# Attention scores of two heads as 64-row tiles, in an encoder layer on one core of a Trainium2 chip

## The chip, the cores and the metric

The kernel runs on one core of one Trainium2 chip. The metric is the device time in microseconds of one execution of the whole program. Shorter is better. The times of several executions are compared by their median, and a profiled execution shows where the time goes.

A core has five engines, each with its own queue of instructions that it works off in order: PE (TensorE, matrix products and transposes), DVE (VectorE), ACT (ScalarE), POOL (GpSimd) and SP (SyncE, which here issues the DMAs). They wait for one another through semaphores. PE multiplies a stationary operand (the weights, loaded by an instruction of its own, shown as PEld) with a moving operand that streams past it, and writes to PSUM, which has eight banks.

## The reference

One layer of an encoder is computed for two groups of 1024 rows, x_prompt and x_sample, with shared weights; everything is in 32-bit floats. Per group:

```python
h = rms_norm(x, norm_g) * (1 + scale) + shift          # scale, shift, gate from silu(c) @ w_ada + b_ada
qa, ka, va, za, qb, kb, vb, zb, ga, gb = split(h @ w_in)
# A: 8 query heads, 2 key/value heads of 64; RMS norm of q and k per head, 2-D rotary positions
oa = softmax(qa @ ka.T / 8) @ va * silu(za)             # query head j uses key/value head j // 4
# B: 4 heads, two 64-wide softmax maps each, values of 128
ob = (softmax(q0 @ k0.T / 8) - lam * softmax(q1 @ k1.T / 8)) @ vb
ob = rms_norm(ob, subln_g) * (1 - lam_init) * silu(zb)
merged = sigmoid(ga) * (oa @ w_proj_a) + sigmoid(gb) * (ob @ w_proj_b)
y = x + gate * (merged @ w_out)
```

The score products contract over 64 numbers only, the width of a head.

## The kernel before

PE multiplies 32-bit numbers in a rounded format here (float32r in the code). To keep the accuracy, the kernel splits an operand into an exact high part and a low part, the rest: `x = hi + lo`. A product of two split operands is then hi·hi + hi·lo + lo·hi, three matmuls that add up in one PSUM bank. The projections (`proj_tt`, L432, and `z_gen`, L594) do this over eight chunks of 128 rows.

**Scores before.** A head is 64 wide, so its high and low parts together fill 128 partitions. `pairs_T` (L472) transposes a pair of heads (L479) and writes, for each head, one tile with the high part on one half of the partitions and the low part on the other: two ACT copies (L481) and two DVE subtractions (L482), each on 64 partitions. For the keys `swap_halves` (L496) makes a second copy in which the halves have changed places, with POOL (L501). `softmax_unit` (L607) then takes 128 queries of one head: for each half of the 1024 keys it multiplies the stacked query tile with the stacked keys (hi·hi + lo·lo, L617) and with the swapped ones (hi·lo + lo·hi, L618), both over all 128 rows of the array, into one bank of the pool `ps_s`, which has two buffers. DVE takes the row maximum from it (L619), ACT the exponential and its sum (L620). The two halves are brought together by small operations on DVE, ACT and POOL (L621 to L625).

**What follows the scores.** `a_scores` (L628) and `b_scores` (L641) scale the exponentials (L637, L653, L660) into tiles of the pool `ppool`, six buffers of 128 x 1024. `pT_pieces` (L665) transposes them on PE (L671), splits them (L674, L675), and the value products follow (L686 and L687 for branch A, L713 for B). `attention` (L739) computes the scores of a unit, then the values of the unit before. In branch A a unit is one head and 256 queries, in branch B one head (two maps) and 256 queries.

**The order of the work.** Generators yield after each step, and `weave` (L60) lays several of them beside each other at given shares: in six phases per group (two for branch A, four for B) the attention runs beside the projections that the next phase needs and beside pieces of the gate paths (`z_gen`), which keep PE supplied. A scheduler in the tile framework then takes the instructions, with their dependences, and fixes the final order of each engine's queue when the program is built. In group 0, phase 5, `gate_gen` (L375) adds small products with only two output rows (L383).

`load_w` (L154) brings 256 columns of a weight matrix with one DMA for each half (L162) where they are contiguous, and splits them on ACT and POOL. Two such weight tiles are held.

Of the kernel before, what the change touches and what calls it, by code (L numbers as in the profile page):

```python
# [78 lines left out]
def kernel(ctx: ExitStack, tc: tile.TileContext, t: dict):  # L79
# [74 lines left out]
    def load_w(pieces):  # L154
        """pieces(half) -> the columns of four contraction chunks, 256 in all"""
# [32 lines left out]
    def row_scale(xt):  # L188
        """1 / rms of the rows"""
# [117 lines left out]
    def mod_rows():  # L307
        """the second group's shift and scale, as rows in DRAM"""
# [14 lines left out]
    def ht0(ht):  # L323
        """the modulation of the first group's transposed rows, and their split"""
# [128 lines left out]
    def rope(x3, s3, cos, sin, half):  # L453
        """x3 = x3*cos + swap(x3)*sin; s3 is scratch"""
# [15 lines left out]
    LO, HI = slice(0, 64), slice(64, 128)  # L470

    def pairs_T(x3, even, odd):  # L472
        """Transpose pairs of heads; the exact parts of the first of each pair go to even (high
        part in the lower partitions), those of the second to odd (high part in the upper ones)."""
# [5 lines left out]
        for dst, hi, lo in ((even, LO, HI), (odd, HI, LO)):  # L480
            nc.scalar.activation(dst[hi], ps[hi], AF.Copy)  # L481
            nc.vector.tensor_tensor(out=dst[lo], in0=ps[hi], in1=dst[hi].bitcast(F32), op=ALU.subtract)  # L482
# [13 lines left out]
    def swap_halves(dst, srcs, tq):  # L496
        """dst = the sources with their partition halves swapped, over half of the positions"""
        sl = slice(tq * 512, (tq + 1) * 512)
        for i, src in enumerate(srcs):
            for a, b in ((LO, HI), (HI, LO)):  # L500
                nc.gpsimd.tensor_scalar(  # L501
                    out=dst[a, i, sl], in0=src[b, sl].bitcast(F32),
                    scalar1=1.0, scalar2=1.0, op0=ALU.mult, op1=ALU.mult,
                )

# [3 lines left out]
    def kva_gen(ht, out):  # L509
        w = kva_w.pop() if kva_w else load_w(w_cols(w_in, (C_KA, 256)))  # L510
        k1, k2 = v2(utile()), v2(utile())
        va = utile().rearrange("p (n k d) -> p n k d", n=NTT, k=2)
        out["k1"], out["k2"], out["va"] = k1, k2, va
# [11 lines left out]
        def back(tt, x3):  # L525
            sl = slice(tt * P, (tt + 1) * P)
            pairs_T(x3, k1[:, 0:1, sl], k1[:, 1:2, sl])
            if tt % 4 == 3:
                swap_halves(k2, (k1[:, 0], k1[:, 1]), tt // 4)
# [3 lines left out]
    def qa_gen(ht, out, half):  # L533
        w = load_w(w_cols(w_in, (C_QA + half * 256, 256)))
# [15 lines left out]
    def qkb_gen(ht, out, h):  # L550
        w = load_w(w_cols(w_in, (C_QB + h * P, P), (C_KB + h * P, P)))
        qk, k2 = (v2(utile()), v2(utile())), v2(utile())
        out[h] = (qk, k2)
# [8 lines left out]
        def back(tt, x3):  # L562
            sl = slice(tt * P, (tt + 1) * P)
            pairs_T(x3, qk[0][:, :, sl], qk[1][:, :, sl])
            if tt % 4 == 3:
                swap_halves(k2, (qk[0][:, 1], qk[1][:, 1]), tt // 4)
# [40 lines left out]
    def softmax_unit(q, k1, k2, qt, pt, f):  # L607
        """Scores of 128 queries: each half of the keys goes to pt as exp(scores - the half's maximum);
        f gets the factor of each half that makes the row's softmax of it"""
        qsl = q[:, qt * P : (qt + 1) * P]  # L610
        m = tiny.tile([P, 2], F32, tag="m", name=nm("m"))
        su = tiny.tile([P, 2], F32, tag="su", name=nm("su"))
        mm = tiny.tile([P, 1], F32, tag="mm", name=nm("mm"))
        for n in range(2):
            s = ps_s.tile([P, 512], F32, tag="s", name=nm("s"))
            sl = slice(n * 512, (n + 1) * 512)
            nc.tensor.matmul(s, qsl, k1[:, sl], start=True, stop=False)  # L617
            nc.tensor.matmul(s, qsl, k2[:, sl], start=False, stop=True)  # L618
            nc.vector.tensor_reduce(out=m[:, n : n + 1], in_=s, axis=AX.X, op=ALU.max, negate=True)  # L619
            nc.scalar.activation(pt[:, sl], s, AF.Exp, bias=m[:, n : n + 1], accum_out=su[:, n : n + 1])  # L620
        nc.vector.tensor_tensor(out=mm, in0=m[:, 0:1], in1=m[:, 1:2], op=ALU.min)  # L621
        nc.scalar.activation(f, m, AF.Exp, scale=-1.0, bias=mm)  # L622
        nc.gpsimd.tensor_tensor(out=su, in0=su, in1=f, op=ALU.mult)  # L623
        nc.gpsimd.tensor_tensor(out=mm, in0=su[:, 0:1], in1=su[:, 1:2], op=ALU.add)
        nc.gpsimd.tensor_tensor(out=mm, in0=mm, in1=mone, op=ALU.pow)  # L625
        return mm

    def a_scores(u):  # L628
        q, k1, k2, pr = u["q"], u["k1"], u["k2"], u["pr"]
        u["p"] = []  # L630
        for i in range(2):
            pt = ptile()
            f = tiny.tile([P, 2], F32, tag="r", name=nm("r"))
            r = softmax_unit(q, k1, k2, pr * 2 + i, pt, f)
            for n in range(2):
                half = pt[:, n * 512 : (n + 1) * 512]
                nc.gpsimd.tensor_scalar(out=half, in0=half, scalar1=f[:, n : n + 1], scalar2=r, op0=ALU.mult, op1=ALU.mult)  # L637
            u["p"].append(pt)
            yield 1

    def b_scores(u):  # L641
        u["p"] = []
        for i in range(2):
            qt = u["pr"] * 2 + i
            p0, p1 = ptile(), ptile()
            f0 = tiny.tile([P, 2], F32, tag="r", name=nm("r"))
            f1 = tiny.tile([P, 2], F32, tag="r", name=nm("r"))
            for m, (pt, f) in enumerate(((p0, f0), (p1, f1))):
                r = softmax_unit(u["qk"][m][:, 0], u["qk"][m][:, 1], u["k2"][:, m], qt, pt, f)
                if m == 0:  # L650
                    for n in range(2):
                        half = p0[:, n * 512 : (n + 1) * 512]
                        nc.gpsimd.tensor_scalar(  # L653
                            out=half, in0=half, scalar1=f0[:, n : n + 1], scalar2=r, op0=ALU.mult, op1=ALU.mult
                        )
                yield 1
            nc.gpsimd.tensor_scalar(out=f1, in0=f1, scalar1=r, scalar2=nlam, op0=ALU.mult, op1=ALU.mult)  # L657
# [5 lines left out]
            u["p"].append(p0)  # L663

    def pT_pieces(u):  # L665
        for cc in range(4):
            ps = tbank().rearrange("p (c n) -> p c n", c=2)
            for c in range(2):
                k = (cc * 2 + c) * P
                for i in range(2):  # L670
                    nc.tensor.transpose(ps[:, c, i * P : (i + 1) * P], u["p"][i][:, k : k + P], ident)  # L671
# [6 lines left out]
    def a_values(u):  # L678
        acc = ps_a.tile([P, 512], F32, tag="a", name=nm("a"))[:, :256]
        prev = None  # L680

        def pv(cc, th, tl):
            for c in range(2):
                k = cc * 2 + c
                lt = u["v"](k)
# [3 lines left out]
        for piece in pT_pieces(u):  # L689
# [7 lines left out]
        j = u["j"]  # L697
# [4 lines left out]
        dma(u["od"][pr // 2][a, (pr % 2) * 256 : (pr % 2 + 1) * 256], o[a])  # L702
        yield 1

    def b_values(u):
# [12 lines left out]
        for piece in pT_pieces(u):  # L718
# [30 lines left out]
    def gated_gen(st, br, hf, oT):  # L749
        """a branch's output, normalised and gated, and its split"""  # L750
# [32 lines left out]
    def merge_gen(st, oT, mT):  # L783
        """the branches' projections, merged by their gates"""
# [31 lines left out]
    def out_gen(g, mT):  # L816
        """the output projection and the residual"""
# [163 lines left out]
```

## Time and profile before

| | us |
|---|---|
| median of 3 runs | 2159.86 |
| lowest and highest run | 2158.99, 2160.14 |
| profiled execution, its span | 2162.3 |

All the rows shown below are from the profiled execution, whose span is the time from its first to its last instruction; what lies around the span isn't recorded. Busy time is the union of the recorded durations of an engine's instructions. A group row gives line, engine, operation, output and inputs by their names in the program, shapes, the count, then busy time in us and the mean of one in ns, and then the idle time of the engine just before these instructions with what ended it. A row of a timeline gives the start and the length in us of several equal instructions in a row, and their number behind the x. In a row of stretches stand begin and end, length, and the busy time of PE, PEld, DVE, ACT and POOL with their counts, then the granted clock as a share, the share of the DMA engines, and GB/s.

### The profile page before, as it was taken

How to read it: one execution, taken by the hardware profiler on the slowest of the kernel's cores; microseconds unless marked ns; L12 is line 12 of the kernel's file. 1: busy time of each engine (PE TensorE's matmuls, PEld its weight loads, DVE VectorE, ACT ScalarE, POOL GpSimd, SP SyncE). 2: the span in 40 equal slices, each digit the busy share in tenths (PEclk: the TensorE clock that was granted, in tenths of full speed). 3: DMA queues.
4: the chain of work that ended last, by engine and by line, in shares of the span. 5: the costliest groups of instructions: out<-in, count | busy, mean ns of one | idle time of the engine just before them, and what ended most of it. 6: DMA issues, size and time to landing. Idle time of an engine off the chain costs nothing.

```text
span 2162.3 us, 36893 instructions
## 1 busy us (share of the span) xinstructions
PE 2063.4 (95%) x13098; PEld 1829.6 (85%) x13098; DVE 1479.4 (68%) x3042; ACT 1166.9 (54%) x2758; POOL 1140.2 (53%) x1778
## 2 busy tenths in 40 slices
PE   5789999999999999999999999999999999999999
PEld 2778879889888977878998798988988798887899
DVE  6887676777887675566737876587788747547542
ACT  6445656766665554743224566676666545556410
POOL 5655555675775564423415666566667646552210
PEclk9899999999999999999999999999999999999999
DMA  8121021110100123564441112111120112228432
GB/s 278 49 62 44 26 59 36 33 54 22 56 21 23 56 79 117 167 229 146 153 123 42 36 41 61 36 33 35 41 63 13 43 53 67 76 85 269 134 115 88
DMA packets 148036, 171.15 MB, mean 79 GB/s; under 512 B 15454, under 2 KB 112766, under 8 KB 147852
## 3 DMA queue, kind: packets, MB, share of 16 engines
q1 hardware_dynamic: 147852, 168.80, 24.7%
q8 instruction: 103, 1.69, 0.3%
q14 instruction: 81, 0.66, 0.1%
HBM read 126.80 MB, written 41.96 MB: 78 GB/s over the span
## 4 chain that ended last, share of the span: by engine, by line
PE 42%; DVE 6%; POOL 3%; issue 2%; ACT 2%; DMA 2%; SPq 0%; POOLq 0%; ACTq 0%; DVEq 0%
PE f L594 9%; PE f L432 7%; PE f L832 4%; PE t L832 4%; PE f L803 3%; PE t L803 3%; PE t L671 3%; PE s L617 2%; PE s L618 2%; PE a L687 1%; PE a L713 1%; PE a L686 1%; DVE m L619 1%; DMA p<-zd 1%; DVE sq L464 1%
## 5 line engine op out<-in xcount | busy, mean ns | idle before, releaser
L594 PE MATMUL f<-u,w 128*128 128x512 f32 x2280 | 577.3, 397 | 2.0 <-DVE u L579 1.3
L620 ACT ACTIVATE p<-s,m 128x512 f32<-128x512 f32 x512 | 350.8, 686 | 269.0 <-DVE m L619 240.7
L594 PEld LDWEIGHTS f<-u,w 128*128 128x128 f32 x2280 | 420.0, 190 | 87.7 <-issue 1.8
L432 PE MATMUL f<-w,u 128*128 128x256 f32 x3456 | 479.9, 287 | 10.3 <-DVE u L520 3.9
L432 PEld LDWEIGHTS f<-w,u 128*128 128x128 f32 x3456 | 450.4, 192 | 27.9 <-DVE u L520 4.3
L168 POOL TENSOR_TENSOR w<-st,w 128x1024 fp32r<-128x1024 f32 x116 | 287.4, 2494 | 317.4 <-ACT w L167 304.0
L619 DVE TENSOR_REDUCE m<-s 128x1 f32<-128x512 f32 x512 | 347.5, 685 | 111.2 <-PE s L618 107.0
L675 DVE TENSOR_TENSOR th<-t,th 128x512 fp32r<-128x512 f32 x384 | 260.7, 686 | 161.7 <-ACT th L674 158.6
L674 ACT ACTIVATE th<-t 128x512 fp32r<-128x512 f32 x384 | 224.2, 596 | 89.3 <-PE a L687 46.6
L623 POOL TENSOR_TENSOR su<-su,r 128x2 f32<-128x2 f32 x256 | 52.8, 206 | 382.2 <-ACT r L622 350.4
L671 PE MATMUL t<-ident,p 128*128 128x128 f32 x1536 | 240.1, 275 | 9.2 <-DVE th L675 5.0
L637 POOL TENSOR_SCALAR p<-p,r,mm 128x512 f32<-128x512 f32 x256 | 203.1, 802 | 12.0
L671 PEld LDWEIGHTS t<-ident,p 128*128 128x128 f32 x1536 | 184.1, 142 | 26.1 <-issue 5.4
L618 PE MATMUL s<-u,u 128*128 128x512 f32 x512 | 204.6, 400 | 0.0
L167 ACT ACTIVATE w<-st 128x1024 fp32r<-128x1024 f32 x116 | 117.4, 1053 | 74.1 <-PE f L832 41.5
L625 POOL TENSOR_TENSOR mm<-mm,mone 128x1 f32<-128x1 f32 x256 | 145.8, 570 | 18.8
L686 PE MATMUL a<-th,u 128*128 128x256 f32 x512 | 139.8, 293 | 1.5 <-DVE oo L700 1.4
L687 PE MATMUL a<-th,u 128*128 128x256 f32 x512 | 137.2, 293 | 3.5 <-DVE th L675 3.5
L713 PE MATMUL a<-th,u 128*128 128x256 f32 x768 | 128.9, 291 | 5.8 <-DVE th L675 5.3
L660 DVE SCALAR_TENSOR_TENSOR p<-p,r,p 128x512 f32<-128x512 f32 x128 | 106.6, 873 | 34.6 <-POOL r L657 33.9
L713 PEld LDWEIGHTS a<-th,u 128*128 128x128 f32 x768 | 110.8, 193 | 20.4 <-DVE th L675 9.6
L617 PE MATMUL s<-u 128*128 128x512 f32 x256 | 110.1, 430 | 5.5 <-ACT p L620 4.9
(153 smaller groups left out, 3400.0 us busy)
## 6 DMA issues: line engine op xcount, KB each, us to landing
st<-in_w_in_dram SPq DMA_DIRECT2D x68, 512.0 KB, 3.9
zd<-ev SPq DMA_DIRECT2D x96, 256.0 KB, 2.0
p<-zd SPq DMA_DIRECT2D x96, 256.0 KB, 3.9
u<-in_w_ada_dram SPq DMA_DIRECT2D x8, 1024.0 KB, 11.6
st<-in_w_in_dram SPq DMA_DIRECT2D x32, 256.0 KB, 3.4
p<-od SPq DMA_DIRECT2D x32, 256.0 KB, 3.6
st<-in_w_out_dram SPq DMA_DIRECT2D x16, 512.0 KB, 5.5
p<-in_x_prompt_dram SPq DMA_DIRECT2D x8, 512.0 KB, 9.5
```

The source lines that it names most:

```text
L168: nc.gpsimd.tensor_tensor(out=wl, in0=st, in1=wh.bitcast(F32), op=ALU.subtract)
L432: nc.tensor.matmul(ps, lt[c][:, sl], w[:, c, wi, :], start=(k == 0), stop=(k == 23))
L594: nc.tensor.matmul(ps, w[:, c, wi, e * P : (e + 1) * P], rt[c], start=(k == 0), stop=(k == 23),)
L618: nc.tensor.matmul(s, qsl, k2[:, sl], start=False, stop=True)
L619: nc.vector.tensor_reduce(out=m[:, n : n + 1], in_=s, axis=AX.X, op=ALU.max, negate=True)
L620: nc.scalar.activation(pt[:, sl], s, AF.Exp, bias=m[:, n : n + 1], accum_out=su[:, n : n + 1])
L637: nc.gpsimd.tensor_scalar(out=half, in0=half, scalar1=f[:, n : n + 1], scalar2=r, op0=ALU.mult, op1=ALU.mult)
L671: nc.tensor.transpose(ps[:, c, i * P : (i + 1) * P], u["p"][i][:, k : k + P], ident)
L674: nc.scalar.activation(th, ps, AF.Copy)
L675: nc.vector.tensor_tensor(out=tl, in0=ps, in1=th.bitcast(F32), op=ALU.subtract)
L713: nc.tensor.matmul(acc, u["v"][:, k, s, :], rt[:, c, :], start=(k == 0 and s == 0 and rt is th), stop=(k == 7 and s == 1),)
L832: nc.tensor.matmul(ps, m[:, mi, (tt % 4) * P : (tt % 4 + 1) * P], w[:, c, wi, :], start=(k == 0), stop=(k == 23),)
```

## The change

The scores of two heads are computed together, each on one half of the array's rows (a row tile of 64 rows). `pairs_T` writes the high parts of a transposed pair of heads to one tile and the low parts to another, with one ACT and one DVE instruction over 128 partitions; the swapped copies of the keys and `swap_halves` are gone. `softmax_pair` takes two heads, or the two maps of a head in branch B, and issues three products for each, alternating between the halves; a helper makes the scheduler keep these six in order. In branch A the two heads of a pair are j and j + 4, which use key/value head 0 and 1, so `qa_gen` fetches its columns in four pieces of 64. A unit of branch A holds two heads now, and `attention` lays the values of the unit before between the steps of the scores.

```diff
-    def pairs_T(x3, even, odd):
+    def pairs_T(x3, hi, lo):
...
-        for dst, hi, lo in ((even, LO, HI), (odd, HI, LO)):
-            nc.scalar.activation(dst[hi], ps[hi], AF.Copy)
-            nc.vector.tensor_tensor(out=dst[lo], in0=ps[hi], in1=dst[hi].bitcast(F32), op=ALU.subtract)
+        nc.scalar.activation(hi, ps, AF.Copy)
+        nc.vector.tensor_tensor(out=lo, in0=ps, in1=hi.bitcast(F32), op=ALU.subtract)
...
     def qa_gen(ht, out, half):
-        w = load_w(w_cols(w_in, (C_QA + half * 256, 256)))
+        cols = [C_QA + (j + 4 * kv) * HD for j in (half * 2, half * 2 + 1) for kv in range(2)]
+        w = load_w(w_cols(w_in, *[(c, HD) for c in cols]))
...
-            if tt % 4 == 3:
-                swap_halves(k2, (qk[0][:, 1], qk[1][:, 1]), tt // 4)
...
+    def after(inst, prev):
+        if prev is not None:
+            tc.add_manual_dep(
+                inst.ins, prev.ins.name,
+                mybir.DependencyInfo(mybir.DependencyClass.NoSync, mybir.DependencyReason.SCHED_ONLY),
+                reason="row tiles side by side",
+            )
+
+    def softmax_pair(q, k, qt, pts, fs):
+        qsl = slice(qt * P, (qt + 1) * P)
...
         for n in range(2):
-            s = ps_s.tile([P, 512], F32, tag="s", name=nm("s"))
+            ss = [ps_s.tile([P, 512], F32, tag="s", name=nm("s")) for _ in range(2)]
             sl = slice(n * 512, (n + 1) * 512)
-            nc.tensor.matmul(s, qsl, k1[:, sl], start=True, stop=False)
-            nc.tensor.matmul(s, qsl, k2[:, sl], start=False, stop=True)
-            nc.vector.tensor_reduce(out=m[:, n : n + 1], in_=s, axis=AX.X, op=ALU.max, negate=True)
-            nc.scalar.activation(pt[:, sl], s, AF.Exp, bias=m[:, n : n + 1], accum_out=su[:, n : n + 1])
+            last = None
+            for i, (a, b) in enumerate(((0, 0), (0, 1), (1, 0))):
+                for m in (1, 0):
+                    pp = slice(m * 64, m * 64 + 64)
+                    mm = nc.tensor.matmul(ss[m], q[a][pp, qsl], k[b][pp, sl], start=(i == 0), stop=(i == 2))
+                    after(mm, last)
+                    last = mm
+            for m in range(2):
+                h = slice(n, n + 1)
+                nc.vector.tensor_reduce(out=ms[m][:, h], in_=ss[m], axis=AX.X, op=ALU.max, negate=True)
+                nc.scalar.activation(pts[m][:, sl], ss[m], AF.Exp, bias=ms[m][:, h], accum_out=su[m][:, h])
+            if n == 0:
+                yield 1
...
     def a_scores(u):
-        q, k1, k2, pr = u["q"], u["k1"], u["k2"], u["pr"]
-        u["p"] = []
+        u["p"] = [], []
         for i in range(2):
-            pt = ptile()
...
+            pts, fs = (ptile(), ptile()), factors()
+            rs = yield from softmax_pair(u["q"], u["k"], u["pr"] * 2 + i, pts, fs)
+            for m in range(2):
+                normalise(pts[m], fs[m], rs[m])
+                u["p"][m].append(pts[m])
             yield 1
...
     def a_values(u):
+        for m in range(2):
+            yield from a_value(u, m)
...
     def attention(units, scores, values):
-        prev = None
+        prev, steps = iter(()), 0
         for u in units:
-            yield from scores(u)
-            if prev is not None:
-                yield from values(prev)
-            prev = u
-        yield from values(prev)
+            done = 0
+            for i, _ in enumerate(scores(u)):
+                yield 1
+                n = (i + 1) * steps // 4 - done
+                done += n
+                for _ in islice(prev, n):
+                    yield 1
+            yield from prev
+            prev, steps = values(u), u["steps"]
+        yield from prev
```

More of the change, by code (lines that the diff above doesn't have):

```diff
@@ L494, in pipelined @@
             yield 1
[L496 to L504, printed above, removed]
     def v2(u):
@@ L510, in kva_gen @@
         w = kva_w.pop() if kva_w else load_w(w_cols(w_in, (C_KA, 256)))
-        k1, k2 = v2(utile()), v2(utile())
+        kk = v2(utile())
         va = utile().rearrange("p (n k d) -> p n k d", n=NTT, k=2)
-        out["k1"], out["k2"], out["va"] = k1, k2, va
+        out["k"], out["va"] = kk, va
         def front(tt, ps):
@@ L551, in qkb_gen @@
         w = load_w(w_cols(w_in, (C_QB + h * P, P), (C_KB + h * P, P)))
-        qk, k2 = (v2(utile()), v2(utile())), v2(utile())
-        out[h] = (qk, k2)
+        qk = v2(utile()), v2(utile())
+        out[h] = qk
         def front(tt, ps):
@@ L604, in z_gen @@
                 yield 1
[L607 to L613, printed above, removed]
+    def after(inst, prev):
[5 more added lines that the diff above has]
+            )
@@ L614, in softmax_unit @@
+    def softmax_pair(q, k, qt, pts, fs):
+        qsl = slice(qt * P, (qt + 1) * P)
+        ms = [tiny.tile([P, 2], F32, tag="m", name=nm("m")) for _ in range(2)]
+        su = [tiny.tile([P, 2], F32, tag="su", name=nm("su")) for _ in range(2)]
         for n in range(2):
-            s = ps_s.tile([P, 512], F32, tag="s", name=nm("s"))
+            ss = [ps_s.tile([P, 512], F32, tag="s", name=nm("s")) for _ in range(2)]
             sl = slice(n * 512, (n + 1) * 512)
-            nc.tensor.matmul(s, qsl, k1[:, sl], start=True, stop=False)
@@ L618, in softmax_unit @@
[L618 to L624, printed above, removed]
@@ L625, in softmax_unit @@
-        nc.gpsimd.tensor_tensor(out=mm, in0=mm, in1=mone, op=ALU.pow)
-        return mm
+            last = None
[9 more added lines that the diff above has]
+                nc.scalar.activation(pts[m][:, sl], ss[m], AF.Exp, bias=ms[m][:, h], accum_out=su[m][:, h])
@@ new lines, in softmax_pair @@
+            if n == 0:
+                yield 1
+        rs = []
+        for m in range(2):
+            mm = tiny.tile([P, 1], F32, tag="mm", name=nm("mm"))
+            nc.vector.tensor_tensor(out=mm, in0=ms[m][:, 0:1], in1=ms[m][:, 1:2], op=ALU.min)
+            nc.scalar.activation(fs[m], ms[m], AF.Exp, scale=-1.0, bias=mm)
+            nc.gpsimd.tensor_tensor(out=su[m], in0=su[m], in1=fs[m], op=ALU.mult)
+            nc.gpsimd.tensor_tensor(out=mm, in0=su[m][:, 0:1], in1=su[m][:, 1:2], op=ALU.add)
+            nc.gpsimd.tensor_tensor(out=mm, in0=mm, in1=mone, op=ALU.pow)
+            rs.append(mm)
@@ L628, in a_scores, with normalise, factors @@
+        return rs
+    def normalise(pt, f, r):
+        for n in range(2):
+            half = pt[:, n * 512 : (n + 1) * 512]
+            nc.gpsimd.tensor_scalar(out=half, in0=half, scalar1=f[:, n : n + 1], scalar2=r, op0=ALU.mult, op1=ALU.mult)
+    def factors():
+        return [tiny.tile([P, 2], F32, tag="r", name=nm("r")) for _ in range(2)]
     def a_scores(u):
-        q, k1, k2, pr = u["q"], u["k1"], u["k2"], u["pr"]
-        u["p"] = []
+        u["p"] = [], []
         for i in range(2):
-            pt = ptile()
[L633 to L638, printed above, removed]
+            pts, fs = (ptile(), ptile()), factors()
[3 more added lines that the diff above has]
+                u["p"][m].append(pts[m])
@@ L643, in b_scores @@
         for i in range(2):
[L644 to L657, printed above, removed]
+            (p0, p1), (f0, f1) = (ptile(), ptile()), factors()
+            r0, r1 = yield from softmax_pair(u["q"], u["k"], u["pr"] * 2 + i, (p0, p1), (f0, f1))
+            normalise(p0, f0, r0)
+            nc.gpsimd.tensor_scalar(out=f1, in0=f1, scalar1=r1, scalar2=nlam, op0=ALU.mult, op1=ALU.mult)
             for n in range(2):
@@ L663, in b_scores, with pT_pieces @@
             u["p"].append(p0)
-    def pT_pieces(u):
+            yield 1
+    def pT_pieces(p):
         for cc in range(4):
@@ L670, in pT_pieces @@
                 for i in range(2):
-                    nc.tensor.transpose(ps[:, c, i * P : (i + 1) * P], u["p"][i][:, k : k + P], ident)
+                    nc.tensor.transpose(ps[:, c, i * P : (i + 1) * P], p[i][:, k : k + P], ident)
             hl = tpool.tile([P, 2, 2, 256], F32R, tag="th", name=nm("th"))
@@ L678, in a_values, with a_value @@
     def a_values(u):
+        for m in range(2):
+            yield from a_value(u, m)
+    def a_value(u, m):
         acc = ps_a.tile([P, 512], F32, tag="a", name=nm("a"))[:, :256]
@@ L684, in pv @@
                 k = cc * 2 + c
-                lt = u["v"](k)
+                lt = u["v"][:, k, m, :]
                 nc.tensor.matmul(acc, lt, th[:, c, :], start=(k == 0), stop=False)
                 nc.tensor.matmul(acc, lt, tl[:, c, :], start=False, stop=(k == 7))
-        for piece in pT_pieces(u):
+        for piece in pT_pieces(u["p"][m]):
             if prev is not None:
@@ L696, in a_values @@
         o = mtile("oo", [P, 256])
-        j = u["j"]
+        j = u["j"] + 4 * m
         a, b = (slice(0, 64), slice(64, 128)) if j % 2 == 0 else (slice(64, 128), slice(0, 64))
@@ L701, in a_values @@
         pr = u["pr"]
-        dma(u["od"][pr // 2][a, (pr % 2) * 256 : (pr % 2 + 1) * 256], o[a])
+        dma(u["od"][j // 2][pr // 2][a, (pr % 2) * 256 : (pr % 2 + 1) * 256], o[a])
         yield 1
@@ L716, in pv @@
                     )
-        for piece in pT_pieces(u):
+        for piece in pT_pieces(u["p"]):
             if prev is not None:
@@ L856, in a_units @@
     def a_units(st, half):
-        for i in (0, 2, 1, 3):
-            j = half * 4 + i
+        for i in range(2):
             for pr in range(4):
-                kv = j // 4
                 yield {
-                    "q": st["qa"][half][i % 2][:, i // 2],
-                    "k1": st["k1"][:, kv], "k2": st["k2"][:, kv],
-                    "v": (lambda k, kv=kv: st["va"][:, k, kv, :]),
-                    "pr": pr, "j": j, "od": st["od"][j // 2],
+                    "q": [q[:, i] for q in st["qa"][half]], "k": [st["k"][:, i] for i in range(2)],
+                    "v": st["va"], "pr": pr, "j": half * 2 + i, "od": st["od"], "steps": 10,
                 }
@@ L869, in b_units @@
         for pr in range(4):
-            qk, k2 = st["qkb"][h]
+            qk = st["qkb"][h]
             yield {
-                "qk": qk, "k2": k2, "v": st["vb"][h], "pr": pr, "h": h,
-                "od": st["od"][4 + h], "ss": st["ssB"],
+                "q": [u[:, 0] for u in qk], "k": [u[:, 1] for u in qk],
+                "v": st["vb"][h], "pr": pr, "h": h,
+                "od": st["od"][4 + h], "ss": st["ssB"], "steps": 5,
             }
```

6 lines of the change are left out of this document (2 added, 4 removed).

## The prediction

> **What bounds the kernel now.** I read the totals of the page first, then the busy time by stretch, then the chain that ended last, and only then single instructions.
>
> ```profile
> span 2162.3 us, 36893 instructions
> PE 2063.4 (95%) x13098; PEld 1829.6 (85%) x13098; DVE 1479.4 (68%) x3042; ACT 1166.9 (54%) x2758; POOL 1140.2 (53%) x1778
> PEclk9899999999999999999999999999999999999999
> PE 42%; DVE 6%; POOL 3%; issue 2%; ACT 2%; DMA 2%; SPq 0%; POOLq 0%; ACTq 0%; DVEq 0%
> ```
>
> TensorE is busy 95% of the span at nearly the full granted clock; no other engine passes 68%. The chain names PE far ahead of any other engine. The attention of the two groups, where the change lies, fills four stretches:
>
> ```profile
> 127.00:520.00 393.00, 376.04 (x2457) 338.40 (x2457) 281.12 (x590) 249.39 (x617) 232.40 (x382) 0.98 0.15 43
> 520.00:860.00 340.00, 328.95 (x2054) 282.70 (x2052) 250.29 (x540) 193.05 (x500) 210.84 (x374) 0.98 0.18 56
> 1180.00:1541.00 361.00, 349.75 (x2315) 313.54 (x2314) 267.17 (x586) 239.03 (x601) 221.96 (x372) 1.00 0.14 41
> 1541.00:1945.00 404.00, 394.98 (x2429) 348.63 (x2428) 276.79 (x582) 226.40 (x571) 242.71 (x420) 1.00 0.17 54
> ```
>
> The columns after the length are PE, weight loads, DVE, ACT, POOL, clock. PE is idle there for 17.0 + 11.1 + 11.3 + 9.0 = 48 us of 1498; DVE has 423 us free. So a microsecond more or less of PE in these stretches is about one in the end, and work on DVE, ACT and POOL is nearly free.
>
> "Busy" overstates a matmul, because its recorded length contains the tail that overlaps the next one. What it occupies is the distance from start to start in a long series:
>
> ```profile
> 1761.79 3.04 PE L432 MATMUL f<-w,u 128*128 128x256 f32 x24
> 1764.67 0.38 PE L479 MATMUL f<-ident,raw 128*128 128x128 f32 x2
> ...
> 1765.81 5.63 PE L594 MATMUL f<-u,w 128*128 128x512 f32 x24
> 1771.28 0.39 PE L617 MATMUL s<-u 128*128 128x512 f32 x1
> ```
>
> (1764.67 - 1761.79) / 24 = 0.120 us for 256 columns, (1771.28 - 1765.81) / 24 = 0.228 us for 512. I call 0.228 us a slot. Each matmul has a weight load of its own, which in such a series is hidden under the matmul before.
>
> ```profile
> L618 PE MATMUL s<-u,u 128*128 128x512 f32 x512 | 204.6, 400 | 0.0
> L617 PE MATMUL s<-u 128*128 128x512 f32 x256 | 110.1, 430 | 5.5 <-ACT p L620 4.9
> L617 PE MATMUL s<-u,u 128*128 128x512 f32 x256 | 109.8, 429 | 5.3 <-ACT p L620 5.3
> ```
>
> The scores are 512 + 512 = 1024 slots, 233 us. They hardly wait.
>
> **The change part by part.** *Products.* Two heads' score tiles needed 2 x 2 = 4 slots. Now they are 3 products for each head, on half of the array's rows. If both halves run at once, that is 3 slots, and 256 such groups would save 256 x 0.228 = 58 us. But the compiled order of PE does not keep the six together. The helper `after` fixes their order, not their neighbourhood. In that order the 1536 row-tile matmuls stand in 492 runs with full-array work between: 223 runs of one, 194 of five, 35 of six, 40 others. The usual picture is the first matmul of the upper head alone, then projections or values, then the other five. A run takes as many slots as its fuller half has matmuls: 1 for a lone one, 3 for five, 3 for six. Over all runs that is 984 slots, not 768: 40 fewer than before, a gain of 9.1 us.
>
> *Entering and leaving the row-tile mode.* The trace has no row tile of 64, but it has an interruption of the same kind: the gate's products (L383) write two output rows, on a narrow column tile, between full-array matmuls.
>
> ```profile
> 818.26 0.38 PE L713 MATMUL a<-th,u 128*128 128x256 f32 x1
> 818.57 1.03 PE L383 MATMUL f<-st,cT 128*2 128x256 f32 x4
> 819.53 0.98 PE L713 MATMUL a<-th,u 128*128 128x256 f32 x6
> ...
> 821.66 0.40 PE L617 MATMUL s<-u 128*128 128x512 f32 x1
> 821.89 0.40 PE L618 MATMUL s<-u,u 128*128 128x512 f32 x1
> 822.22 0.59 PE L383 MATMUL f<-st,cT 128*2 128x256 f32 x2
> 822.74 0.50 PE L617 MATMUL s<-u 128*128 128x512 f32 x1
> 823.08 0.40 PE L618 MATMUL s<-u,u 128*128 128x512 f32 x1
> 823.31 0.85 PE L594 MATMUL f<-u,w 128*128 128x512 f32 x3
> ...
> 830.27 3.62 PE L383 MATMUL f<-st,cT 128*2 128x256 f32 x16
> 833.82 0.44 PE L671 MATMUL t<-ident,p 128*128 128x128 f32 x2
> ```
>
> Sixteen in a row take 3.55 us, so one takes 0.215 with a share of one exit. Then: from L618 to L383 at 822.22 pass 0.33 us instead of 0.23, so entering costs 0.10. The two L383 take 0.52 instead of 0.43, so leaving costs 0.09. The first full matmul afterwards takes 822.74 to 823.08 = 0.34 instead of 0.23: its 128-column weights were not loaded ahead, 0.11. The trip from 818.26 to 819.53 gives the same: 1.27 us, less 0.12 and 4 x 0.215, is 0.29. On entry L383 loads two columns only, so that load is not seen; a row tile loads 128, and I add the 0.10 that the exit shows. One run then costs 0.29 + 0.10 = 0.39 us, and 492 runs 191.9 us. Where a run is followed by a transpose (126 of them), the exposed load is shorter:
>
> ```profile
> L594 PEld LDWEIGHTS f<-u,w 128*128 128x128 f32 x2280 | 420.0, 190 | 87.7 <-issue 1.8
> L671 PEld LDWEIGHTS t<-ident,p 128*128 128x128 f32 x1536 | 184.1, 142 | 26.1 <-issue 5.4
> ```
>
> 0.19 against 0.14, so 126 x 0.05 = 6.3 us less. In the 60 runs with as many matmuls on one half as on the other, the second half starts one load (0.107) late and ends late: 6.4 us more. A pair needs two loads per slot, 2 x 0.107 = 0.214 against 0.228, which just fits.
>
> What I do not know is whether a row tile pays this price of a column tile. Bounds per run: nothing, if row halves are only masks; 0.19, if both loads hide under the emptying; 0.39, if all is as with L383. I take 0.39, the only switch that the trace prices. The Trainium skill speaks against the change here: TensorEngine Tiling (Array Packing), section Key Properties, says that changing the tiling mode, not only the tile, drains TensorE; it gives no price. By that rule row tiles pay as column tiles do and the sum stands; by the rows alone, read narrowly, they might pay nothing, which is a rival below.
>
> *What leaves the other engines.*
>
> ```profile
> L482 DVE TENSOR_TENSOR u<-f,u 64x256 fp32r<-64x256 f32 x160 | 67.2, 422 | 20.2 <-ACT u L481 16.0
> L481 ACT ACTIVATE u<-f 64x256 fp32r<-64x256 f32 x160 | 59.5, 374 | 21.2 <-DVE u L482 15.8 <-PE f L479 3.6
> L501 POOL TENSOR_SCALAR u<-u 64x512 fp32r<-64x512 f32 x80 | 51.8, 651 | 10.4 <-ACT u L481 4.5 <-DVE ss L444 0.2 <-POOL mm L624 0.2
> ```
>
> The swapped copies go: 80 x 0.65 = 52 us of POOL. Each transposed pair of blocks is split by one ACT and one DVE instruction over 128 partitions instead of two over 64, which halves these counts: some 30 us of ACT and 34 of DVE in the shapes shown. None of it sets the end: PE's work covers it. I count nothing; at most it takes away part of the 48 us of idle PE.
>
> *What moves.* A unit of branch A now holds two heads, its values stand between its neighbour's scores, and transposes and value products keep their numbers. The query weights of branch A come as four DMAs of 64 columns where one brought 256, for 4 weight tiles of two halves: 24 more issues on SP's queue, in pieces a quarter as wide.
>
> ```profile
> st<-in_w_in_dram SPq DMA_DIRECT2D x68, 512.0 KB, 3.9
> st<-in_w_in_dram SPq DMA_DIRECT2D x32, 256.0 KB, 3.4
> ```
>
> Halving the width (the 256 KB rows) did not lengthen a landing. If a quarter doubled it, a tile came 4 us later, once for each of 4 tiles: 0 to 16 us. The tiles are fetched a whole projection (8 x 24 x 0.120 = 23 us) ahead, which hides it: nothing.
>
> *A wait that changes place.* There are two score banks. Before, one was filled while the other was reduced; now a pair takes both and hands back both.
>
> ```profile
> L620 ACT ACTIVATE p<-s,m 128x512 f32<-128x512 f32 x512 | 350.8, 686 | 269.0 <-DVE m L619 240.7
> L619 DVE TENSOR_REDUCE m<-s 128x1 f32<-128x512 f32 x512 | 347.5, 685 | 111.2 <-PE s L618 107.0
> ```
>
> A maximum and two exponentials in a row make 0.685 + 2 x 0.686 = 2.06 us until both banks are free. The waiting matmul holds up all of PE's queue behind it, transposes and projections too. But a half of a pair comes every 1498 / 256 = 5.9 us, and full-array work stands between. Bounds: -25 us (half of the 48 us idle goes, since PE is later and its feeders are not) to +25 us (0.1 us for each of 256 halves). I take zero.
>
> *Sum.* 191.9 - 6.3 + 6.4 - 9.1 = +183 us on the profiled 2162.3, that is 2345. That execution is 2.4 us longer than the median of the runs, 2159.86, so I forecast 2343 us, 8.5% slower; its own range with the waits is 2315 to 2370.
>
> **The rivals.**
>
> Halves run one after the other (13%). Then a run has as many slots as matmuls, 1536 in all: 552 x 0.228 = 126 us more, 2469. For it: no row here shows two matmuls at once. Against: the two halves share neither operand rows nor a result bank.
>
> Weights not loaded ahead inside a run (10%). If a half can load only when its own matmul is over, every repeated slot (984 - 492 = 492) starts 0.107 late: +53 us, 2396. Against it: L594's series keeps 0.228 with a load recorded at 0.19 each. The Trainium skill, TensorE: Matmul & The Clock Gate, section The mechanism, says that a weight load overlaps running matmuls only when the row group differs, which leads here; the same section also allows a background buffer, and the series of this trace agrees with the latter.
>
> Loads hide under the emptying (10%). 0.19 for each run: 492 x 0.19 = 93.5, less 9.1: 2244.
>
> No price for the switch (9%), the case on the other side. Row halves are only masks, each run costs nothing, and the 40 saved slots remain: 2162.3 - 9.1 - 2.4 = 2151, faster. It decides below 9.1 / 492 = 18 ns for a run. For it: the rows show a column tile, whose outputs change; a row tile keeps all 128 outputs. Against: a full-array matmul uses both halves, so it must wait for both anyway.
>
> Score banks bind (6%). If PE had nothing else between, each half would wait one exponential longer, 256 x 0.69 = 177 us, on top of the switches: 2520. Against it: the 5.9 us per half.
>
> **How the numbers follow.** The forecast has 52%. The range 2240 to 2470 takes in the dear and the half-priced switch, late weights and serial halves; it leaves out the free switch (9%) and the banks (6%), and tails. A measurement of this kernel tells about 0.2% from no change, 4 us. Only the free switch can end faster or level: faster 8%, level 3%, slower 89%.
>
> **What would show it.** Right: a distance of about 0.33 us from the last full matmul to the first row tile; a lone row tile followed by full work some 0.4 us later than its slot; in a run of five the two halves starting about 0.11 apart and about 0.23 per pair; PE still busy, DVE's share lower. Wrong: distances of 0.23 at the run's ends (free switch), 0.23 between all five (serial halves), 0.33 (late weights), or new idle time before the scores released by ACT's exponential (banks).

## The result, and the profile after

The changed kernel takes 2370.9 us, median of four runs (2367.5 to 2374.8), against 2160.0 for the kernel before. The ratio is 1.098 (95% interval 1.096 to 1.099): 9.8% slower. The forecast was 2343, with a range of 2240 to 2470.

First the page of the changed kernel: span, busy time, granted clock by fortieth of the span, and the chain that ended last.

```profile
span 2373.0 us, 37595 instructions
PE 2261.5 (95%) x13610; PEld 1838.0 (77%) x13610; DVE 1357.6 (57%) x2930; ACT 1122.5 (47%) x2652; POOL 1051.0 (44%) x1698
PEclk8999999998999999979999999999899999997999
PE 85%; DVE 5%; ACT 3%; DMA 3%; POOL 2%; issue 2%; SPq 1%; ACTq 0%; POOLq 0%; DVEq 0%
```

PE is still busy 95%, of a longer span. DVE fell from 68% to 57% and POOL from 53% to 44%: the removed copies and splits are really gone, but the end did not wait for them. PEld keeps its busy time (1829.6 us before, 1838.0 now), so its share of the longer span falls from 85% to 77%.

Where the 211 us came from is seen in four stretches of the span: the scores of the first group, what lies between, the scores of the second group, and the rest. First the kernel before, then the changed one.

```profile
128.10:898.50 770.40, 742.39 (x4709) 653.11 (x4708) 552.20 (x1163) 469.49 (x1169) 462.11 (x788) 0.98 0.17 53
898.50:1179.80 281.30, 272.15 (x1782) 249.44 (x1781) 177.74 (x336) 104.58 (x197) 97.44 (x92) 0.99 0.47 149
1179.80:1944.00 764.20, 743.94 (x4736) 661.37 (x4735) 543.50 (x1168) 464.66 (x1170) 463.77 (x791) 1.00 0.15 48
1944.00:2162.30 218.30, 211.75 (x1330) 191.54 (x1328) 108.49 (x179) 64.83 (x93) 43.91 (x24) 0.99 0.48 153
```

```profile
119.10:1019.75 900.65, 872.62 (x5140) 682.59 (x5140) 507.32 (x1127) 449.32 (x1131) 429.37 (x757) 0.98 0.16 50
1019.75:1283.95 264.20, 242.56 (x1607) 224.36 (x1605) 166.36 (x325) 99.72 (x183) 84.62 (x85) 0.94 0.46 145
1283.95:2159.30 875.35, 858.01 (x5101) 680.15 (x5101) 490.99 (x1121) 449.75 (x1132) 432.75 (x757) 0.98 0.14 46
2159.30:2373.00 213.70, 198.75 (x1244) 180.01 (x1241) 109.54 (x181) 64.05 (x89) 38.77 (x25) 0.95 0.43 140
```

The two attentions grew by 130 and 111 us, nearly all of it PE busy time (+130 and +114). The other stretches became 17 and 5 us shorter. They hold fewer matmuls (1607 instead of 1782, and 1244 instead of 1330), which now run beside the longer attention; the head of the span is 9 us shorter.

One group of six row tiles, in the timeline of PE of the changed kernel (start, length and number of equal instructions in a row):

```profile
818.82 0.40 PE L432 MATMUL f<-w,u 128*128 128x256 f32 x2
819.14 0.49 PE L613 MATMUL s<-u 64*128 64x512 f32 x1
819.56 0.51 PE L432 MATMUL f<-w,u 128*128 128x256 f32 x2
820.00 0.50 PE L613 MATMUL s<-u 64*128 64x512 f32 x1
820.00 0.96 PE L613 MATMUL s<-u,u 64*128 64x512 f32 x4
820.89 2.30 PE L432 MATMUL f<-w,u 128*128 128x256 f32 x17
```

This is the picture that the compiled order promised: one row tile alone, two projections, then five. Two full matmuls (0.24) take 0.32 until the row tile starts: 0.08 to 0.09 for entering. The lone row tile keeps PE for 0.42 instead of 0.228: its weight load and the way out. The next two full matmuls take 0.44: 0.24, the load that could not be made ahead, 0.11, and again 0.09. The five take 0.89 us, which is 3 x 0.228 and the same 0.20; the first of each half starts at 820.00.

The same timeline of the weight loads shows that the second half's load did not queue behind the first's:

```profile
819.56 0.30 PEld L432 LDWEIGHTS f<-w,u 128*128 128x128 f32 x2 [0.24 <-issue]
820.00 0.18 PEld L613 LDWEIGHTS s<-u 64*128 64x128 f32 x1
820.00 0.52 PEld L613 LDWEIGHTS s<-u,u 64*128 64x128 f32 x4
```

The longest waits of PE in the changed kernel (in total, times, longest, in us):

```profile
PE s L613 <- ACT p L619: 20.6, 25, 3.5
PE t L672 <- DVE p L660: 15.5, 4, 12.9
PE t L737 <- ACT at L731: 8.8, 4, 5.0
```

Before, the scores waited half as long for the exponential:

```profile
PE s L617 <- ACT p L620: 10.2, 11, 3.4
```

The 12.9 us of the second row lie behind the last scores of the first group (PE goes on at 1033.3 us), where the order leaves few projections.

### The profile page after: what moved, and what is told of

The parts are those of the page before. It is cut to its first block, busy times and chain, and to the rows that moved or that the text cites. A ratio compares the mean times of both kernels' runs of the same rounds, so it can differ in the third digit from the quotient of the medians.

```text
span 2373.0 us, 37595 instructions
## 1 busy us (share of the span) xinstructions
PE 2261.5 (95%) x13610; PEld 1838.0 (77%) x13610; DVE 1357.6 (57%) x2930; ACT 1122.5 (47%) x2652; POOL 1051.0 (44%) x1698
## 4 chain that ended last, share of the span: by engine, by line
PE 85%; DVE 5%; ACT 3%; DMA 3%; POOL 2%; issue 2%; SPq 1%; ACTq 0%; POOLq 0%; DVEq 0%
PE f L577 22%; PE f L432 18%; PE s L613 12%; PE t L672 7%; PE f L843 4%; PE a L718 4%; PE t L843 3%; PE t L814 3%; PE f L814 3%; PE a L692 3%; PE a L691 3%; ACT p L619 1%; DVE m L618 1%; POOL w L168 1%; PE f L476 1%
## 5 line engine op out<-in xcount | busy, mean ns | idle before, releaser
L577 PE MATMUL f<-u,w 128*128 128x512 f32 x2280 | 599.0, 405 | 0.3 <-ACT raw L440 0.3
L432 PE MATMUL f<-w,u 128*128 128x256 f32 x3456 | 504.8, 292 | 8.4 <-DVE u L335 4.0
L618 DVE TENSOR_REDUCE m<-s 128x1 f32<-128x512 f32 x512 | 330.8, 684 | 196.6 <-PE s L613 195.8
L613 PE MATMUL s<-u,u 64*128 64x512 f32 x1280 | 307.3, 441 | 7.9 <-ACT p L619 7.7
L636 POOL TENSOR_SCALAR p<-p,r,mm 128x512 f32<-128x512 f32 x384 | 295.8, 782 | 1.3
L672 PE MATMUL t<-ident,p 128*128 128x128 f32 x1536 | 259.2, 286 | 23.6 <-DVE p L660 15.5
L613 PEld LDWEIGHTS s<-u,u 64*128 64x128 f32 x1280 | 144.5, 188 | 69.2 <-issue 25.1
L691 PE MATMUL a<-th,u 128*128 128x256 f32 x512 | 147.9, 304 | 2.1 <-DVE oo L705 1.2
L692 PE MATMUL a<-th,u 128*128 128x256 f32 x512 | 143.2, 304 | 0.5 <-DVE th L676 0.5
L718 PE MATMUL a<-th,u 128*128 128x256 f32 x768 | 137.2, 302 | 5.7 <-DVE th L676 3.0
L629 POOL TENSOR_TENSOR mm<-mm,mone 128x1 f32<-128x1 f32 x256 | 136.2, 549 | 0.2
L718 PEld LDWEIGHTS a<-th,u 128*128 128x128 f32 x768 | 111.7, 198 | 29.7 <-issue 10.7
L445 POOL TENSOR_SCALAR ss<-ss 128x4 f32<-128x4 f32 (+1 forms) x112 | 23.7, 211 | 250.3 <-DVE ss L444 234.7
```

The source lines that it names most:

```text
L432: nc.tensor.matmul(ps, lt[c][:, sl], w[:, c, wi, :], start=(k == 0), stop=(k == 23))
L577: nc.tensor.matmul(ps, w[:, c, wi, e * P : (e + 1) * P], rt[c], start=(k == 0), stop=(k == 23),)
L613: mm = nc.tensor.matmul(ss[m], q[a][pp, qsl], k[b][pp, sl], start=(i == 0), stop=(i == 2))
L618: nc.vector.tensor_reduce(out=ms[m][:, h], in_=ss[m], axis=AX.X, op=ALU.max, negate=True)
L672: nc.tensor.transpose(ps[:, c, i * P : (i + 1) * P], p[i][:, k : k + P], ident)
L691: nc.tensor.matmul(acc, lt, th[:, c, :], start=(k == 0), stop=False)
```

## The experiments

Each was timed in three rounds beside the kernel before, whose median lay between 2160.0 and 2163.4. A run of row tiles, below, is a series of them in PE's queue with no full-array matmul between; a trip is one entry into the row-tile mode and one exit; a slot is 0.228 us, as in the prediction.

**The change without its row tiles.** The units of two heads, the order and the two banks stay; the products are the old ones.

```diff
-            for i, (a, b) in enumerate(((0, 0), (0, 1), (1, 0))):
-                for m in (1, 0):
...
+            for m in range(2):
+                nc.tensor.matmul(ss[m], q[m][:, qsl], k[m][:, sl], start=True, stop=False)
+                nc.tensor.matmul(ss[m], q[m][:, qsl], k2[m][:, sl], start=False, stop=True)
```

> The changed kernel with its units of two heads, its order of scores and values, its query columns and its two score banks, but with the old products: high and low parts stacked over 128 partitions, swapped copies of the keys, two full-array matmuls for each score tile, no row tiles. Theory (the 211 us are the 492 trips into and out of the row-tile mode, and little else): about 2165 us, between 2155 and 2195, since the end of each group's attention, which the changed kernel leaves without projections beside it, may stay. Rival (the new units and the pair of score banks cost the time): 2300 us or more.

2180.7 us, ratio 1.010 (1.008 to 1.012). So the row tiles make 2370.9 - 2180.7 = 190 of the 211 us, and everything else 21. (The splits and swapped copies of the old products are back here too, so the 190 is the row tiles together with the work that they save on the other engines.) Its stretches, cut as before:

```profile
128.40:905.70 777.30, 746.88 (x4702) 652.27 (x4701) 542.88 (x1162) 466.54 (x1168) 458.30 (x787) 0.98 0.17 53
905.70:1194.70 289.00, 276.95 (x1789) 253.57 (x1788) 177.64 (x336) 108.59 (x201) 99.09 (x94) 0.98 0.45 145
1194.70:1953.20 758.50, 744.22 (x4723) 658.48 (x4722) 527.00 (x1170) 470.75 (x1172) 456.78 (x785) 1.00 0.16 49
1953.20:2182.20 229.00, 216.63 (x1342) 193.66 (x1340) 111.93 (x177) 70.29 (x97) 48.54 (x29) 0.99 0.44 142
```

The two attentions together take as long as before (+6.9 and -5.7). The new units and the pair of score banks cost nothing there; the loss lies in the stretches behind the attentions, +7.7 and +10.7.

**One score tile for the pair.** A tile of two banks keeps the six together: 259 runs instead of 492.

```diff
-    ps_s = ent(tc.tile_pool(name="ps_s", bufs=2, space=PSUM))
+    ps_s = ent(tc.tile_pool(name="ps_s", bufs=1, space=PSUM))
...
-            ss = [ps_s.tile([P, 512], F32, tag="s", name=nm("s")) for _ in range(2)]
+            wide = ps_s.tile([P, 2, 512], F32, tag="s", name=nm("s"))
+            ss = [wide[:, m] for m in range(2)]
```

> The changed kernel with one score tile of two banks for the pair, in place of two tiles of one bank: both halves become free together, and in the compiled order the six row-tile matmuls stay together. 259 runs instead of 492, 774 slots instead of 984. Theory (a run costs 0.39 us, a slot 0.228): 2371 - 233 x 0.39 - 210 x 0.228 = 2371 - 91 - 48 = 2232 us, give or take 20, for no projection stands beside the last scores of a group here. Rival (a run costs nothing, the waits for the score banks do): the bank is handed back later, so no gain or a loss, 2371 or more.

2431.5 us, ratio 1.126 (1.124 to 1.128): the theory's number was missed by 200 us. The page and the waits of PE:

```profile
PE 2179.2 (90%) x13610; PEld 1823.0 (75%) x13610; DVE 1388.8 (57%) x2930; ACT 1144.4 (47%) x2656; POOL 1066.0 (44%) x1698
```

```profile
PE s L614 <- ACT p L620: 77.7, 47, 4.2
PE t L673 <- DVE p L661: 55.2, 14, 15.7
```

PE is busy 82 us less than in the changed kernel, but idle 252 us instead of 112, and its mean clock fell from 0.968 to 0.942. To see whether trips or the tile did it, the same tile was put under the old products.

> The kernel of the first experiment (full-array products, no row tiles) with the one score tile of two banks from the second. Theory (in the second experiment fewer trips and slots were gained, and the wait for a tile that is handed back as a whole took more than that): 2431 + 57 for the slots - 259 x 0.39 = 2387, between 2330 and 2420, with idle time before the scores released by ACT. Rival (the single tile costs nothing, runs of six cost more than runs of one and five): about 2181.

2478.1 us, ratio 1.147 (1.145 to 1.149): the tile alone costs 2478.1 - 2180.7 = 297 us. Its page and waits:

```profile
PE 2194.6 (89%) x13098; PEld 1909.7 (77%) x13098; DVE 1476.1 (60%) x3042; ACT 1187.4 (48%) x2766; POOL 1117.1 (45%) x1778
```

```profile
PE s L627 <- ACT p L632: 108.3, 63, 3.4
PE t L685 <- DVE p L673: 35.1, 13, 11.8
```

PE is idle 281 us where the first experiment has 102, and the wait for the exponential alone rose from 14.6 to 108.3. So the one tile, handed back as a whole, was the cause of the miss. It costs more than was expected, though, and it does not add up with the other terms: with this tile, the row tiles are 47 us faster than the stacked products, where the sum says 44 slower. Single runs have the old price in the timeline (a run of six takes 0.89 us), but where PE waits as long as here, its occupied time is not the price of the change. What makes the 47 us wasn't followed up.

**The order of the six.** First the three of one half, then the three of the other.

```diff
-            for i, (a, b) in enumerate(((0, 0), (0, 1), (1, 0))):
-                for m in (1, 0):
+            for m in (1, 0):
+                for i, (a, b) in enumerate(((0, 0), (0, 1), (1, 0))):
```

> The changed kernel with the six matmuls in another order: first the three of the upper half, then the three of the lower one. The compiled order has 492 runs as before, of 1536 row-tile matmuls, but 1346 slots instead of 984, as the halves can no longer be side by side. Theory (matmuls on the two halves run at once): 362 x 0.228 = 83 us more, 2453 us. Rival (they never overlapped): no change, 2371.

2400.0 us, ratio 1.111 (1.109 to 1.113): 29 us slower than the changed kernel, not 83. The 1346 slots count the fuller half of each run, as in the prediction. 339 of the 492 runs are now three matmuls of one half, and all 51 runs of six have the three of the upper half ahead of the three of the lower. One run of each kind, in branch B:

```profile
584.11 0.82 PE L672 MATMUL t<-ident,p 128*128 128x128 f32 x6
584.85 0.51 PE L613 MATMUL s<-u 64*128 64x512 f32 x2
585.19 0.63 PE L613 MATMUL s<-u,u 64*128 64x512 f32 x4
585.75 1.20 PE L577 MATMUL f<-u,w 128*128 128x512 f32 x4
...
590.13 0.49 PE L613 MATMUL s<-u 64*128 64x512 f32 x1
590.47 0.63 PE L613 MATMUL s<-u,u 64*128 64x512 f32 x2
591.02 0.98 PE L432 MATMUL f<-w,u 128*128 128x256 f32 x6
```

The three of one half take 0.89 us to the next full matmul, as long as the five of both halves in the changed kernel. So there the halves did run side by side, and the slots of this order are paid. The six take 0.90, also three slots and the 0.20. If they started in the order of the queue they would need five slots, 1.34 us in all. The names show what happened: the first product of each half reads its queries and keys from one tile (`s<-u`), the other two from two (`s<-u,u`). In the queue the two `s<-u` stand first and fourth; here both start ahead of the other four. So these halves ran side by side although their matmuls stand one behind the other.

The end time rose by less than the slots because other losses became smaller:

```profile
PE 2324.6 (97%) x13610; PEld 1881.6 (78%) x13610; DVE 1384.4 (58%) x2930; ACT 1130.1 (47%) x2652; POOL 1054.9 (44%) x1698
```

PE is busy 63 us longer than in the changed kernel but idle 77 us instead of 112, which leaves the 29. That it is 63 and not 83 fits the granted clock, which rose from 0.968 to 0.978: an estimate of 0.010 x 2260 = 23 us less.

**More gate work beside the last scores.** Only the shares of the gate pieces changed.

```diff
-    (11, 7, 4, 3, 4, 11),
-    (9, 6, 6, 4, 8, 7),
+    (9, 6, 3, 2, 3, 22),
+    (7, 5, 5, 3, 7, 21),
```

> The changed kernel with other shares of the gate paths: the pieces of the phases are (9, 6, 3, 2, 3, 22) and (7, 5, 5, 3, 7, 21), so that more of them stand beside the last phase of each group. In the compiled order the last 150 matmuls of a group's attention hold 65 and 55 of the gate paths, where the changed kernel has 21 and 18. 502 runs and 991 slots. Theory (of the 211 us some 28 are the bare end of the attention, where TensorE waits and falls to half its clock): 2371 - 28 + 10 x 0.39 + 7 x 0.228 = 2349, between 2340 and 2360. Rival (that end costs little, since its work has to be done anyway): 2371 to 2380.

2376.4 us, ratio 1.100 (1.097 to 1.102): no gain. Behind the first group's attention PE is now idle 13.5 us instead of 21.6, but behind the second's 22.1 instead of 15.0, and one wait of 11.1 us is left there. So the theory of the bare end finds no support, but the edit relieved only one of the two ends.

**A dose of trips.** The kernel of the first experiment, with a row tile that does no work of the result.

```diff
+            nc.tensor.matmul(ss[0][:, 0:64], q[0][0:64, qsl], k[0][0:64, n * 512 : n * 512 + 64], start=True, stop=True)
             for m in range(2):
                 nc.tensor.matmul(ss[m], q[m][:, qsl], k[m][:, sl], start=True, stop=False)
```

> The kernel of the first experiment (units of two heads, full-array products, no row tiles) with one matmul added ahead of each pair of score tiles: 64 rows, 64 columns, into a score bank that the full product then overwrites, so nothing of the result depends on it. The compiled order holds 256 of them, each alone between full-array work: 256 trips into the mode and out of it, and no row tile that does any of the work. Theory (0.39 us for a trip, plus 0.03 for 64 columns): 2181 + 256 x 0.42 = 2288 us, between 2275 and 2300. Rival (a trip is nearly free, the row-tile kernel loses its time elsewhere): 2181 + 256 x 0.03 = 2189.

2267.5 us, ratio 1.048 (1.045 to 1.050): 87 us for 256 trips, 0.34 us each. Two of them in the timeline of PE:

```profile
701.44 0.29 PE L625 MATMUL s<-u 64*128 64x64 f32 x1
701.66 0.50 PE L627 MATMUL s<-u 128*128 128x512 f32 x1
702.00 0.40 PE L628 MATMUL s<-u,u 128*128 128x512 f32 x1
...
704.68 0.29 PE L625 MATMUL s<-u 64*128 64x64 f32 x1
704.91 0.50 PE L627 MATMUL s<-u 128*128 128x512 f32 x1
705.24 0.39 PE L628 MATMUL s<-u,u 128*128 128x512 f32 x1
```

The row tile of 64 columns keeps PE for 0.22 to 0.23, the full matmul after it for 0.33 to 0.34 instead of 0.228. With 0.09 for entering that is the expected 0.42; the time shows 0.34, so about a fifth fell into waits: PE is idle 89 us here and 102 in the first experiment.

> The dose again, twice as large: ahead of each pair of score tiles two matmuls of 64 columns, one on each half of the rows, both overwritten by the full products. In the compiled order 482 of them stand alone and 15 times two follow one another: 497 trips, about as many as the changed kernel has. The dose of 256 gave 2267 against 2181, 0.34 us a trip. Theory (the price is one of trips, and each is paid): 2181 + 497 x 0.34 = 2350 us, between 2335 and 2390 (0.42 a trip if none of it falls into waits). Rival (the first dose disturbed the order of the work once, the count matters little): 2270 to 2300.

2366.9 us, ratio 1.096 (1.094 to 1.098): 186 us for 497 trips, 0.375 each. This kernel does all its scores on the full array, and the useless trips alone bring it to the time of the changed kernel.

> The first dose with the added matmul on all 128 rows instead of 64: 256 matmuls of 64 columns with weights of their own, also overwritten, and no change of mode. Theory (what costs is the change of mode): each occupies TensorE for its weight load, 0.107 us, less what falls into waits: between 2181 and 2181 + 256 x 0.107 = 2208. Rival (an added matmul and its wait for the score bank cost the 87 us): 2267.

The same added matmul on 128 rows gives 2213.6 us, ratio 1.024 (1.023 to 1.026): 33 us, 0.13 each. That is somewhat above the expected bound of 0.107. The change of mode is the other 87 - 33 = 54 us, 0.21 for each trip.

**Four score banks.** PSUM's eight banks were shared out as 4 for scores, 2 for transposes, 1 for projections, 1 for values.

```diff
-    ps_s = ent(tc.tile_pool(name="ps_s", bufs=2, space=PSUM))
-    ps_t = ent(tc.tile_pool(name="ps_t", bufs=3, space=PSUM))
-    ps_f = ent(tc.tile_pool(name="ps_f", bufs=2, space=PSUM))
+    ps_s = ent(tc.tile_pool(name="ps_s", bufs=4, space=PSUM))
+    ps_t = ent(tc.tile_pool(name="ps_t", bufs=2, space=PSUM))
+    ps_f = ent(tc.tile_pool(name="ps_f", bufs=1, space=PSUM))
```

> The kernel of the first experiment with the PSUM banks shared out in another way: 4 for the scores instead of 2, 2 for transposes instead of 3, 1 for projections instead of 2. A base for the next two. With one bank, each projection has to wait for the copy-out of the one before unless other work stands between, some 0.6 us for 96 gate pieces and 224 projections in the worst case: between 2181 and 2370; I expect 2230. If score banks were what the pair lacked, it would be under 2181.

> The changed kernel with that sharing (4, 2, 1). With four score banks the compiled order has 289 runs and 851 slots where the changed kernel has 492 and 984. Theory (0.39 a run, 0.228 a slot): against the base with the same banks +289 x 0.39 - 173 x 0.228 = 113 - 39 = +73 us, give or take 20; if the base is 2230, 2303. Rival (the row tiles lose by the wait for two banks): level with the base or below it.

> As the last, with one score tile of four banks for both halves of the keys, so that twelve row-tile matmuls follow one another: 160 runs, 778 slots. Theory: against the base with the same banks +160 x 0.39 - 246 x 0.228 = 62 - 56 = +6 us, if nothing waits. Rival, after the second experiment (one tile that is handed back as a whole makes the scores wait for four exponentials): 50 to 200 us more than that, with idle time before the scores released by ACT.

The base came out at 2561.0 us, ratio 1.184 (1.181 to 1.186), beyond its bounds; the changed kernel with these banks at 2423.4, 1.120 (1.117 to 1.123); and with one tile of four banks at 2435.8, 1.127 (1.123 to 1.130). PE of the base is idle 339 us, 47.6 of them for the DVE split behind the one projection bank alone, so it is no base for the price of a trip. The theory had both row-tile kernels above it, by 73 and 6 us; they are 138 and 125 below, with 220 and 268 us of idle PE. What makes that difference wasn't followed up. Against the changed kernel, fewer trips (289 and 160) did not pay for the banks.

## Why the prediction was right

*The price of a trip* was read from the narrow column tiles of the gate, and it holds for row tiles: 0.09 to enter, 0.09 to 0.10 to leave, 0.10 to 0.11 for a load at each end. The dose shows it apart from the change: 0.34 to 0.375 us of the end time, 0.42 of PE with the 0.03 for its columns.

*The sum* for the row tiles was +183 us; the first experiment measured 190. With the 21 us of the next point these are the 28 us by which the forecast was short; 2370.9 lies just above the 2315 to 2370 that the prediction gives for its own mechanism. The sum came out that close partly by luck. Without the 6.4 us that fall away below it is +177, and the other 13 us were in no term: PE of the changed kernel is idle 111.5 us against 102.2 in the first experiment, and its mean clock is 0.968 against 0.983. That the order splits the six, so that 984 slots remain and the saving is 9 us, was seen before the run and is seen in the timeline.

*Nothing for the rest* was the term that was mis-sized: zero, with 25 us either way; it measured +21. It lies behind the attentions, not at the score banks, where the wait rose by 10 us only. Its cause stays open; other shares of the gate pieces, tried in the changed kernel only, gained nothing.

*Two small terms* were wrong in their mechanism. The second half does not start one load late: both halves load and start together, so the 6.4 us for it aren't there. The bare end of each group was not foreseen; there the clock falls, to 0.94 and 0.95 in the stretches behind the attentions against 0.99 before.

*The rivals.* Serial halves: the two first matmuls of a run start at the same 0.01 us. Late weights: five take three slots and one trip. Hidden loads and a free switch: each trip pays both loads and both drains. Score banks that bind: not in the changed kernel (20.6 us of waits), but at once when the two banks became one tile (77.7).

## What to carry to other kernels

A row tile is paid by the trip, not by the matmul: here 0.39 us of PE for each run of them, against 0.228 saved when six replace four. Where PE is the bound, a trip has to save 0.39 / 0.228 = 1.7 slots, so by this sum even six that always stayed together would lose (256 x 0.39 = 100 us against 58). No run here shows that: in the three kernels with fewer runs (259, 289 and 160) PE waits much longer, and each of them is faster than its full-array counterpart, though slower than the changed kernel. The sum is borne out only where PE hardly waits, by the first experiment. Count the trips in the compiled order, for an order that is fixed is not a neighbourhood that is kept.

## What the runs showed of the hardware

TensorE took matmuls of the other half ahead of those in front of them: three queued behind three of the upper half ran beside them, six in 0.90 us instead of 1.34. So its queue is not worked off strictly in order, as the description of the engines at the start has it.

The weight loads of the two halves ran at the same time (the first load and the next four are recorded from 820.00, and so are the first matmuls of both halves).

Useless trips left the mean granted clock where it was, 0.986 with 256 of them and 0.984 with 497, against 0.983 without. The changed kernel fell to 0.968, and the two kernels with the single tile of two banks to 0.942 (with row tiles) and 0.934 (without any), where PE is idle 252 and 281 us. So the lower clock goes with the waits, not with the changes of mode.
